# Streaming hybrid attention layer: in the last head unit the sample's tile is projected behind the sixteen token tiles instead of in front of them

## The chip, the core and the metric

The kernel runs on one core of a Trainium2 chip. The time is the device time of one execution in microseconds (us); before the change it is 2286.06 us, the median of three runs (2282.44 to 2286.41). The core has five engines with a queue of instructions each: PE (TensorE, matrix products), DVE (VectorE), ACT (ScalarE), POOL (GpSimd) and SP (SyncE, which here issues nearly all transfers). Each queue is worked off in the order in which the program holds it, and an instruction waits at the head of its queue until what it reads and writes is ready.

## The reference: what is computed

One layer of a streaming encoder. 2048 new token rows of one stream ("the prompt") and 8 x 16 rows of eight running streams ("the sample", 128 rows, which have cached keys and values) are normalised and modulated, and then projected by one wide weight matrix. Two mixers work side by side: differential attention with 4 heads (two softmaxes, the second subtracted with a factor) and stick-breaking attention with 8 heads:

    z     = q . k / 8                     # for keys before the query only
    log_a = log_sigmoid(z) + (reverse running sum of log_sigmoid(-z), without the own key)
    o     = exp(log_a) @ v

Behind them `y = x + gate * (sigmoid(ga) * ((norm(oa) * silu(za)) @ w_branch_a) + sigmoid(gb) * ((ob * silu(zb)) @ w_branch_b)) @ w_out`, normalised once more. The projected keys and values are outputs too, for the sample's rows as for the prompt's.

## The kernel before, in words

**Tiles and units.** The rows are cut into 17 tiles of 128: token tiles 0 to 15 and the sample's tile, which has number `NT` = 16. The heads are dealt to 8 units: even units hold one differential head, odd units two stick-breaking heads. Products are in float16 with a high and a low part, so a full product is three matmuls for each 128 rows of depth.

**Stage 0** (line 944) computes modulation and the normalised rows, and puts them, turned and split, into DRAM (`hT_d`).

**Stage 1** (lines 866 to 1357) goes through a list of steps `(unit, tile)`, `steps` in line 866. For a step two things have to be done.

- *The projection* (`project`, line 402): 24 matmuls of 128x512 (line 423) for q, k, v and the z gate, and in odd units another 24 (line 495) for a part of the merge gates. ACT, DVE and POOL bring the result to memory, split k, v and q, and transfers store z (`z_d`), gates (`g_d`) and outputs. For the sample's tile q, k, v also go to DRAM (`s_d`, lines 479, 480), and that is all that becomes of it in stage 1; a token tile is also turned by PE (`transpose_qk`, line 503, with two copies, lines 518 and 519) for its attention. The rows are fetched one step ahead into three buffers `hs`.
- *The attention* (token tiles only): `scores` (line 632) makes for query tile t one or two pieces of up to 512 keys at a time: two PE products (lines 647, 648), two sigmoids on ACT (line 549, 550, by the helper in line 120), a running product on DVE (line 607), and per 1024 keys a product on POOL (line 629), a cast on ACT (line 561), a difference on DVE (line 562) and a transposing transfer (line 568). `pv` (line 725) multiplies these weights with v on PE (lines 706, 707) at least `PV_LAG` = 2 steps later.

**The order.** All projections stand in one list, `line`: each step gives 24 pieces of two matmuls in odd units, and behind the sixth piece of a step stands the turning of the step before it, if that was a token tile. Before the change a last entry (line 901) turns the last token tile. The loop from line 1330 walks over n, one step of attention after the other. `attention(n)` gives the scores of step n and the v products of a step further back; `take` cuts the next pieces off `line`, so that the projection stands `LEAD` = 5 steps ahead of a pace which is counted in attention time: a token tile counts 0.6 + (t+1)/4, the sample's 0.3. `interleave` (line 92) merges pieces, scores and v products evenly, and the merged order is the program's. When `line` is used up, the entries of `cuts` (`early_work`, line 1306) are dealt out over the iterations that are left: one branch weight, one renaming of buffers (`rest`), `inputs` of the first two output tiles (`first`), four half branch products of tile 0 (`early` 0 to 3) and the transposing transfer of its result (`early` 4). Line 1354 takes the number of entries left over the number of iterations left, rounded up.

**Stage 2** (from line 1360) has output tiles 0 to 14, the sample's and 15. For each: `inputs` (line 1215) loads o, z and g (`hs` buffers 0 and 1 for o and z), takes sigmoids, products, a scale and a split into `hs` buffer 2; a transposing transfer (line 1251); four half branch products of 12 matmuls (line 1262); a second scale, split and transposing transfer (line 1287); two halves of 24 matmuls with `w_out` (line 1399), which is loaded at the start of this stage (line 1211) and kept; the last norm, and the store. The sample's attention over the caches is laid in between, unit by unit (`sample`, line 743).

**What fixes an order.** The helper `act` (line 118) makes every ACT instruction with a table function (sigmoid, exp) follow the one before it in the program. For everything else a planner lays the instructions of each engine out by a timeline of its own, with the program's order as the preference (line 1476: `schedule_with_timeline_sim=True`); waits on buffers and results are added by it. So an instruction can stand in its queue earlier or later than the loop wrote it.

**Buffers that are few.** v: 23 tiles (`V_BUFS`), k: 6 groups of four tiles (`K_BUFS`), turned q: 6 (`Q_BUFS`), PE result banks: 2 for `mm`, 3 for `s`, 1 for `t`, 2 for `o`. The sigmoids of z in `inputs` write the `mm` banks too. The buffers of stage 2 lie where those of stage 1 lay.

Of the kernel before, what the change touches and what calls it, by code (L numbers as in the profile page):

```python
# [32 lines left out]
NT = SEQ // P  # L33
# [77 lines left out]
def layer_kernel(ctx: ExitStack, tc: tile.TileContext, a: dict):  # L111
# [75 lines left out]
    def bank(tag, dt=F32):  # L187
        return ps.tile([P, 512 if dt == F32 else 1024], dt, tag=tag, name=f"ps_{tag}", bufs=BANKS[tag])
# [113 lines left out]
    units = [None] * 8  # L302
# [60 lines left out]
    def finish_unit(u):  # L363

        U = units[u]
        sw, sh = U["sw"], sh_box[0]
        sc = con.tile([P, 7], F32, name=f"usc{u}")

        V.tensor_tensor(out=sc[:, 0:1], in0=U["fsq"], in1=nh2, op=ALU.mult)
        sq = scales(sc[:, 0:1], con, f"sq{u}")  # L370

        V.tensor_tensor(out=sc[:, 1:2], in0=sw[:, 1:2], in1=sh[:, 1:2], op=ALU.mult)
        V.tensor_tensor(out=sc[:, 2:3], in0=sc[:, 1:2], in1=sq[:, 0:1], op=ALU.mult)

        V.tensor_scalar(out=sc[:, 3:4], in0=sq[:, 1:2], scalar1=sq[:, 1:2], scalar2=0.125, op0=ALU.mult, op1=ALU.mult)
        V.tensor_scalar(out=sc[:, 4:5], in0=sc[:, 3:4], scalar1=-1.0, scalar2=None, op0=ALU.mult)

        if U["kind"] == 0:
            V.tensor_tensor(out=sc[:, 5:6], in0=sq[:, 1:2], in1=ls[:, 1:2], op=ALU.mult)
        else:  # L380
            V.tensor_scalar(out=sc[:, 5:6], in0=sq[:, 1:2], scalar1=2.0 ** -STICK, scalar2=None, op0=ALU.mult)
        if "sg" in U:

            V.tensor_tensor(out=sc[:, 6:7], in0=U["sg"][:, 1:2], in1=sh[:, 1:2], op=ALU.mult)
        U["sc"], U["sq"], U["k"], U["v"] = sc, sq, {}, {}
# [11 lines left out]
    def fetch_h(u, t):  # L397
        ahead[u, t] = hs[len(fetched) % 3].bitcast(F16).rearrange("p (f k n) -> p f k n", f=2, n=P)
        fetched.append(t)
        load(out=ahead[u, t], in_=hT_d[t // 4][:, t % 4, :, :, :])  # L400
# [102 lines left out]
    def transpose_qk(U, t):  # L503
        g, i = t // 4, t % 4
        q16, k16 = U.pop(("q16", t)), U.pop(("k16", t))
        pt = bank("t", F16)
        for c in range(2):
            T.transpose(pt[:, c * P : (c + 1) * P], k16[:, c, :, :].rearrange("p f d -> p (f d)"), id16)
        for f in range(2):
            for c in range(2):  # L510
                j = 2 + f * 2 + c
                T.transpose(pt[:, j * P : (j + 1) * P], q16[:, f, c, :, :].rearrange("p r d -> p (r d)"), id16)
        if i == 0:
            U["k"][g] = kvp.tile([P, 2, 512], F16, tag="k", name="k", bufs=K_BUFS)
        U["q", t] = qst = stg.tile([P, 4, P], F16, tag="qst", name="qst", bufs=Q_BUFS)
        kst = U["k"][g][:, :, i * P : (i + 1) * P]
        copy = V.tensor_copy if U["kind"] == 1 else S.copy
        (V.tensor_copy if U["u"] == 0 else copy)(out=kst, in_=pt[:, 0:256].rearrange("p (c n) -> p c n", c=2))
        copy(out=qst, in_=pt[:, 256:768].rearrange("p (j n) -> p j n", j=4))
# [343 lines left out]

        return [lambda x=x: one(*x) for x in srcs]

    steps = [(u, t) for u in range(8) for t in [NT] + list(range(NT))]
    back = []
    spare = norms()
    jobs, done = [], []
# [1 line left out]

    line = []

    def begin(u, t):
        if t == NT:
            if u > 0:
                free.extend(units[u - 1]["bufs"])
            finish_unit(u)

    def projection(m):  # L880
        u, t = steps[m]
        made = []

        def piece(i):
            if i == 0:
                begin(u, t)
                made.extend(project(units[u], t))
            if i == H_AT and not at_hand and m + 1 < len(steps) and steps[m + 1] not in ahead:
                fetch_h(*steps[m + 1])
            made[i]()  # L890

        return [lambda i=i: piece(i) for i in range(12 + 3 * GATES[u][1] // 128)]

    starts = []
    for m in range(len(steps)):
        starts.append(len(line))
        for i, fn in enumerate(projection(m)):
            line.append((m, fn))
            if i == TR_AFTER and m > 0 and steps[m - 1][1] < NT:
                line.append((m - 1, lambda m=m: transpose_qk(units[steps[m - 1][0]], steps[m - 1][1])))  # L900
    line.append((len(steps) - 1, lambda: transpose_qk(units[7], NT - 1)))
    starts.append(len(line))
    at = [0]

# [425 lines left out]
    for n in range(first_step, len(steps) + PV_LAG):  # L1330
        if n < len(steps):
            u, t = steps[n]
# [147 lines left out]
```

## Time and profile before

| what | value |
|---|---|
| time, median of 3 runs | 2286.06 us |
| time of the profiled execution | 2285.48 us |
| its span, first to last instruction | 2283.7 us |
| PE busy | 2085.1 us (91%) |
| DVE busy | 1611.5 us (71%) |
| ACT busy | 1482.6 us (65%) |
| POOL busy | 688.1 us (30%) |
| mean granted PE clock | 0.966 |

A row of the profile's timeline gives start, duration, engine, line of the kernel, operation, the tile that is written and those that are read, shape and count; in square brackets stand the idle time of the engine before it and what ended it. Rows of windows give for a stretch of time the busy time of each engine (with counts), then the granted PE clock as a share of full speed, the busy share of the DMA engines and GB/s. Matmuls are pipelined, so the duration of one is longer than the distance between two.

### The profile page before, as it was taken

Reading aid. Unit: us, or ns where it says so; the run is one execution under the profiler, and the core shown is the slowest. Engines: PE = TensorE matmul, PEld = TensorE weight load, DVE = VectorE, ACT = ScalarE, POOL = GpSimd, SP = SyncE. Lnnn points to the kernel's source line nnn. Section 1 sums busy time; section 2 is a strip of 40 time slices with the busy share of each in tenths; the row PEclk is TensorE's granted clock in tenths of the full one; section 3 lists DMA queues with packets and bytes.
Section 4 is the critical chain, followed back from the end, with each engine's and each line's share of the span. In section 5 each row is a group of like instructions: output and inputs, shape, how many; then the busy total and the mean of one; then the engine's idle time right before and its main releaser. Section 6 shows DMA issues by size and latency. Waiting matters only on the chain. (4 is left out here: it accounts for less than half of the span.)

```text
span 2283.7 us, 40470 instructions
## 1 busy us (share of the span) xinstructions
PE 2085.1 (91%) x14478; PEld 1110.4 (49%) x14478; DVE 1611.5 (71%) x3507; ACT 1482.6 (65%) x2952; POOL 688.1 (30%) x559
## 2 busy tenths in 40 slices
PE   4997999999999999899999989999986799888997
PEld 2554554555555455455545555555543444444443
DVE  4668767789875778987577898776777656565554
ACT  3877677787876777786677777666776544444431
POOL 1522012355301335530032553012344232232321
PEclk7999999999999999999999999999997899999998
DMA  8667658697875778876566886757687989788652
GB/s 295 211 212 187 163 131 220 148 221 155 206 169 124 170 154 199 177 179 131 128 172 142 204 183 154 153 140 163 151 179 173 295 228 262 202 220 211 188 150 65
DMA packets 763754, 411.92 MB, mean 180 GB/s; under 512 B 524986, under 2 KB 708586, under 8 KB 763040
## 3 DMA queue, kind: packets, MB, share of 16 engines
q1 hardware_dynamic: 762474, 408.86, 72.6%
q8 instruction: 113, 1.85, 0.3%
q14 instruction: 89, 0.73, 0.1%
q10 hardware_dynamic: 1078, 0.48, 0.1%
HBM read 211.53 MB, written 72.91 MB: 125 GB/s over the span
## 5 line engine op out<-in xcount | busy, mean ns | idle before, releaser
L423 PE MATMUL ps_mm<-wb,hs 128*128 128x512 f16 x1836 | 460.7, 382 | 0.6 <-DVE v L292 0.5
L629 POOL TENSOR_TENSOR sc_p<-sc_p,sc_n 128x1024 f32<-128x1024 f32 (+8 forms) x160 | 278.1, 1742 | 459.2 <-DVE sc_n L607 451.6
L423 PEld LDWEIGHTS <-hs 128*128 128x128 f16 x2928 | 256.1, 98 | 226.9 <-issue 6.8
L607 DVE TENSOR_TENSOR_SCAN sc_n<-ps_s,sc_n,zero_t 128x512 f32<-128x512 f32 x192 | 245.3, 1278 | 64.4 <-ACT ps_s L120 62.2
L423 PE MATMUL ps_mm<-wa,hs 128*128 128x512 f16 x1092 | 279.4, 380 | 0.0
L647 PE MATMUL ps_s<-k,qst 128*128 128x512 f16 (+3 forms) x640 | 225.9, 354 | 38.3 <-DVE sc_n L607 30.1
L120 ACT ACTIVATE sc_p<-ps_s,usc 128x512 f32<-128x512 f32 (+3 forms) x320 | 202.0, 631 | 85.8 <-PE ps_s L648 55.1
L495 PE MATMUL ps_mm<-wa,hs 128*128 128x512 f16 x1020 | 257.0, 379 | 0.0
L562 DVE TENSOR_TENSOR sc_n<-sc_p,sc_n 128x1024 f16<-128x1024 f32 (+7 forms) x160 | 197.9, 1242 | 41.3 <-ACT sc_n L561 41.2
L648 PE MATMUL ps_s<-k,qst 128*128 128x512 f16 (+3 forms) x640 | 226.2, 354 | 0.0
L1399 PE MATMUL ps_o<-wo,wb 128*128 128x512 f16 x816 | 199.5, 401 | 24.7 <-DMA wb<-wa 22.0
L706 PE MATMUL ps_o<-v,wt 128*128 128x128 f16 x1008 | 175.6, 226 | 27.6 <-DMA wt<-sc_n 27.5
L495 PEld LDWEIGHTS <-hs 128*128 128x128 f16 x1632 | 140.2, 98 | 119.0
L120 ACT ACTIVATE ps_s<-ps_s,usc 128x512 f32<-128x512 f32 (+3 forms) x320 | 193.7, 605 | 0.0
L561 ACT CAST sc_n<-sc_p 128x1024 f16<-128x1024 f32 (+7 forms) x160 | 138.5, 870 | 49.2 <-POOL sc_p L629 49.1
L707 PE MATMUL ps_o<-v,wt 128*128 128x64 f16 x1008 | 158.5, 198 | 0.0
L495 PE MATMUL ps_mm<-wb,hs 128*128 128x512 f16 x612 | 155.9, 379 | 0.0
L706 PEld LDWEIGHTS <-wt 128*128 128x128 f16 x1008 | 99.2, 102 | 102.7 <-DMA wt<-sc_n 38.0
L1399 PEld LDWEIGHTS <-wb 128*128 128x128 f16 x816 | 82.1, 102 | 130.4 <-DMA wb<-wa 26.1
L457 POOL TENSOR_TENSOR rot<-pr,rope 128x256 f32<-128x256 f32 x68 | 63.1, 928 | 247.1 <-ACT pr L437 193.3
L437 ACT ACTIVATE pr<-ps_mm,usc 128x512 f32<-128x512 f32 (+1 forms) x136 | 86.5, 636 | 67.4 <-PE ps_mm L423 67.1
L545 DVE TENSOR_SCALAR_CACHE_REDUCE sc_n<-ps_s,usc 128x512 f32<-128x512 f32 (+3 forms) x148 | 99.0, 669 | 42.4 <-PE ps_s L648 28.2
(336 smaller groups left out, 4346.7 us busy)
## 6 DMA issues: line engine op xcount, KB each, us to landing
hs<-hT_d SPq DMA_DIRECT2D x122, 512.0 KB, 4.2
g_d<-gt SPq DMA_DIRECT2D x68, 256.0 KB, 3.4
out_dram<-pr SPq DMA_DIRECT2D x204, 64.0 KB, 1.8
wa<-g_d SPq DMA_DIRECT2D x25, 512.0 KB, 6.7
wide<-in_w_ada_dram SPq DMA_DIRECT2D x12, 1024.0 KB, 8.4
wa<-in_w_in_dram SPq DMA_DIRECT2D x44, 256.0 KB, 4.7
z_d<-pr SPq DMA_DIRECT2D x136, 64.0 KB, 2.7
o_d<-o SPq DMA_DIRECT2D x136, 64.0 KB, 2.7
```

Source lines behind the costliest of these rows:

```text
L120: i = S.activation(**kw)
L423: T.matmul(box["p"], box["h"][:, hi, k, :], U["w"][k][:, wi, :], start=(n == 0), stop=(n == 3 * KT - 1))
L495: T.matmul(box["g"][:, 0:gw], box["h"][:, hi, k, :], U["wg"][k // per][:, k % per, wi, :], start=(j == 0), stop=(j == 3 * KT - 1))
L561: S.copy(out=hi, in_=src)
L562: V.tensor_tensor(out=lo, in0=src, in1=hi, op=ALU.subtract)
L607: V.tensor_tensor_scan(out=dst[:, lo : lo + n][:, ::-1], data0=src[:, 0:n][:, ::-1], data1=zero_t[:, 0:1].to_broadcast([P, n]), initial=fi ...
L629: G.tensor_tensor(out=p[:, 0:m], in0=p[:, 0:m], in1=n[:, 1 : m + 1], op=ALU.mult)
L647: T.matmul(p[:, 0:n], qst[:, c, :], kk[:, c, 0:n], start=True, stop=False)
L648: T.matmul(p[:, 0:n], qst[:, 2 + c, :], kk[:, c, 0:n], start=False, stop=not diag)
L706: T.matmul(po[:, c * P : (c + 1) * P], wt[:, wj, :], vt[:, c, :, :], start=first, stop=False)
L707: T.matmul(po[:, c * P : c * P + 64], wt[:, nb + wj, :], vt[:, c, 0, :], start=False, stop=last)
L1399: T.matmul(po, st["y"][:, yi * 8 + k, :], wo[j * 4 + k // 2][:, wi, k % 2, :], start=(n == 0), stop=(n == 3 * KT - 1))
```

## The change

The list of steps has the sample's tile first in units 0 to 6, as before, and last in unit 7. `begin`, which frees the buffers of the unit before and makes the scales of the new one, ran when a step was the sample's; it now runs when the unit has no scales yet. As the last step is now the sample's, and behind the sixth piece of that step the turning of token tile 15 is written as for any other step, the extra last entry of `line` goes.

```diff
-    steps = [(u, t) for u in range(8) for t in [NT] + list(range(NT))]
+    steps = [(u, t) for u in range(7) for t in [NT] + list(range(NT))] + [(7, t) for t in range(NT + 1)]
...
-    def begin(u, t):
-        if t == NT:
+    def begin(u):
+        if "sc" not in units[u]:
             if u > 0:
                 free.extend(units[u - 1]["bufs"])
             finish_unit(u)
...
-                begin(u, t)
+                begin(u)
...
-    line.append((len(steps) - 1, lambda: transpose_qk(units[7], NT - 1)))
```

## The prediction

> **What bounds the kernel now.** I read the page's strips first, to find where PE, busy for 91% of the span, is not busy.
>
> ```profile
> span 2283.7 us, 40470 instructions
> ...
> PE   4997999999999999899999989999986799888997
> ...
> PEclk7999999999999999999999999999997899999998
> ```
>
> One slice is 57.1 us. Before slice 30 PE is full; slices 30 and 31 (1713 to 1827 us) are the one hole past the start. Windows of 50 and 20 us place it:
>
> ```profile
> 1600.00:1650.00 50.00, 50.00 (x338) 26.10 (x336) 35.22 (x57) 36.06 (x71) 16.20 (x13) 1.00 0.62 146
> ...
> 1700.00:1720.00 20.00, 12.54 (x94) 6.74 (x93) 17.58 (x19) 18.53 (x30) 13.61 (x7) 0.76 0.82 176
> 1720.00:1740.00 20.00, 10.10 (x76) 5.46 (x77) 19.73 (x25) 18.80 (x29) 7.41 (x4) 0.76 0.66 138
> 1740.00:1760.00 20.00, 13.51 (x96) 7.51 (x95) 14.87 (x24) 6.53 (x10) 8.68 (x5) 0.69 0.99 207
> ...
> 1780.00:1800.00 20.00, 11.83 (x42) 5.02 (x41) 10.57 (x17) 7.06 (x10) 2.81 (x3) 0.66 1.08 291
> ```
>
> Up to 1650 PE is saturated. From 1700 to 1740 DVE (19.73 of 20) and ACT (18.80) are, and PE idles half the time. From 1740 to 1760 nothing is: a chain of waits runs. At 1780 the DMA share is 1.08: stage 2 loads its weights. PE's timeline shows the seams:
>
> ```profile
> 1646.97 2.75 PE L423 MATMUL ps_mm<-wb,hs 128*128 128x512 f16 x12
> ...
> 1687.33 0.60 PE L495 MATMUL ps_mm<-wb,hs 128*128 128x512 f16 x2
> ...
> 1690.22 0.39 PE L512 MATMUL ps_t<-id,qbuf 128*128 128x128 f16 x4
> ...
> 1695.92 0.29 PE L706 MATMUL ps_o<-v,wt 128*128 128x128 f16 x1 [3.78 <-DMA wt<-sc_n]
> ...
> 1747.03 0.29 PE L706 MATMUL ps_o<-v,wt 128*128 128x128 f16 x1 [5.63 <-DMA wt<-sc_n]
> ...
> 1749.35 1.01 PE L1262 MATMUL ps_mm<-wa,wb 128*128 128x512 f16 x2 [0.86 <-DVE hs L1236]
> ...
> 1763.00 0.22 PE L706 MATMUL ps_o<-v,wt 128*128 128x128 f16 x1
> ...
> 1763.08 0.22 PE L706 MATMUL ps_o<-v,wt 128*128 128x128 f16 x1
> 1763.14 0.19 PE L707 MATMUL ps_o<-v,wt 128*128 128x64 f16 x1
> 1765.42 0.59 PE L1262 MATMUL ps_mm<-wa,wa 128*128 128x512 f16 x2 [2.08 <-DVE wa L1264]
> ```
>
> The last projection (1687.33) and the last turning (1690.22) end the cover; behind them attention of tiles 13 to 15 is alone, with waits for its weights. The half products of output tile 0 begin at 1749.35, the last v product ends at 1763.3.
>
> **What the change does to the order.** Attention time of a unit is 0.3 + 16 x 0.6 + 34 = 43.9, so 2.58 for each of 17 steps. Before, behind tile 12 there remain 4.1 + 4.35 + 4.6 = 13.05, or 5.05 steps: `line` stands at 136 - 5.05 + 5 = 135.95. Of the last step's 26 entries 25 are taken; tile 13 gets one, the turning of tile 15. After, 0.3 more remains (5.17 steps): 135.83, so 21 of 25 entries, and tile 13 gets the last four pieces of the sample, 8 matmuls. As the pace is counted in attention time, moving the sample costs or wins 0.116 of a step here, not a whole one. `cuts` begin at the same tile (14) but have five iterations instead of four, as one with no attention is left at the end: 9 entries go as 2, 2, 2, 2, 1 instead of 3, 2, 2, 2. The inputs of output tile 0 move from 0.83 of tile 14 to 0.25 of tile 15, those of tile 1 from 0.25 to 0.75 of tile 15; the half products move by one place, and the last transposing transfer of tile 0 stands behind everything.
>
> **T1, 8 matmuls into the hole.** Twelve take 2.75 us; less the 0.38 us tail of one, 11 distances are 2.37, so 0.2155 us each. Eight are 1.7 us which leave the saturated stretch for one in which PE idles 20 - 12.54 of 20 us. The turning goes the other way: four small ones take 0.39, one alone 0.22 (line 647 at 1523.59 below), so 0.057 apart, and six 0.3 us. -1.4 us; 0 if PE's idle time there is not used. What hides them is the wait of 3.78 us. The Trainium skill ("TensorE: Matmul & The Clock Gate", section "Part 1: The HAM clock gate") says that PE runs at half rate after about 3.4 us of idleness; the clock of 0.76 in the window agrees. By that rule the eight take 3.4 us in the hole, and were the hole not there, T1 would be +2.0 instead of -1.4.
>
> **T2, tile 15's two copies out of DVE's stretch.** The same pair in an earlier tile:
>
> ```profile
> 1525.22 0.27 DVE L518 COPY k<-ps_t 128x256 f16<-128x256 f16 x1
> ...
> 1525.60 0.42 DVE L519 COPY qst<-ps_t 128x512 f16<-128x512 f16 x1
> ```
>
> They move to tile 12, where PE is the bound. -0.7 to 0; I take -0.3, as DVE is near its bound only from 1700. The sample's projection leaves no k, v or q to be split, and its five stores are off any path; the count of matmuls and transfers is unchanged.
>
> **T3, the seam to unit 7.**
>
> ```profile
> 1517.09 0.38 PE L647 MATMUL ps_s<-k,qst 128*128 128x512 f16 x1
> ...
> 1523.59 0.22 PE L647 MATMUL ps_s<-k,qst 128*128 128x128 f16 x1
> ...
> 1533.16 0.27 PE L647 MATMUL ps_s<-k,qst 128*128 128x256 f16 x1 [0.27 <-DVE sc_n L655]
> ...
> 1542.68 0.23 PE L702 MATMUL ps_o<-v,wt 128*128 128x128 f16 x1 [1.84 <-DMA wt<-sc_n]
> ```
>
> Between the last scores of unit 6 (1517.09) and the first of unit 7 (1523.59) lies the step without scores. After, tile 0's scores stand in that iteration, and the v products of unit 6's last tile come one token tile later. PE's two waits, 0.27 and 1.84 us, can go or double: -2.1 to +2.1. I take -1.0, since the transfer waited for gets a tile more time. v tiles are no new wait: 16 of unit 6 and 6 of unit 7 are held at once, 22 of 23.
>
> **T4, the inputs of output tile 0, later.** The rows of ACT, DVE and SP:
>
> ```profile
> 1716.67 1.12 ACT L120 ACTIVATE ps_mm<-hs 128x512 f32<-128x512 f32 x2
> ...
> 1720.54 0.69 ACT L120 ACTIVATE sc_p<-ps_s,usc 128x512 f32<-128x512 f32 x1
> ...
> 1726.09 1.16 ACT L120 ACTIVATE ps_mm<-hs 128x512 f32<-128x512 f32 x2
> 1727.13 2.04 ACT L120 ACTIVATE wa<-wa 128x1024 f32<-128x1024 f32 x2
> ...
> 1736.51 0.78 ACT L120 ACTIVATE sc_p<-ps_s,usc 128x512 f32<-128x512 f32 x1
> ```
> ```profile
> 1734.90 3.02 DVE L292 SCALAR_TENSOR_TENSOR hs<-hs,su,hs 128x1024 f16<-128x1024 f32 x1
> ...
> 1753.09 1.28 DVE L292 SCALAR_TENSOR_TENSOR hs<-hs,su,hs 128x1024 f16<-128x1024 f32 x1
> ...
> 1777.37 0.74 DVE L292 SCALAR_TENSOR_TENSOR wa<-wa,sy,wa 128x512 f16<-128x512 f32 x1
> ```
> ```profile
> 1713.28 7.18 SPq L568 DMA_TRANSPOSE wt<-sc_n  x3
> 1720.57 1.10 SPq L1219 DMA_DIRECT2D hs<-z_d  x1
> ...
> 1739.99 0.93 SPq L1218 DMA_DIRECT2D hs<-o_d  x1
> ...
> 1753.23 1.97 SPq L568 DMA_TRANSPOSE wt<-sc_n  x1
> ...
> 1759.42 4.31 SPq L1211 DMA_DIRECT2D x<-in_w_out_dram  x2
> ...
> 1782.74 5.91 SPq L1287 DMA_TRANSPOSE wb<-wa  x1
> ```
>
> `act` ties all sigmoids to the program's order. Three pairs of tiles 14 and 15 (from 1720.54 to the next inputs at 1726.09, 5.5 us) now stand ahead of tile 0's sigmoids: 1716.67 becomes 1722.2. Tile 1's 3 us (1726.09 to 1729.17) now stand before the pair at 1736.51, so at 1733.5; the sum ahead of the last two pairs is the same, and they stay. Behind tile 0's sigmoids run scale, split (to 1737.92), load of tile 1's o into the buffer that it frees (1739.99), its products, and so the banks for the first half product (1749.35). Moved by 5.5 us this starts at 1754.9. The four halves are 48 x 0.2155 = 10.3 us, to 1765.2 against 1763.3, where they have v products among them that can now run in the gap ahead. So 1.9 us at the seam. Behind it tile 0's second split ends at 1778.11, while SP issues its transfer (L1287) only at 1782.74: 4.6 us of slack. 0 to +5.5; I take +1.5, near the 1.9, little of it absorbed.
>
> A second split of the same size took 1.28 us and this one 3.02, with a POOL product beside it from 1734.01. The Trainium skill ("SBUF — State Buffer", section "SBUF: two separate sides") holds that DVE and POOL share a port pair that one locks for a whole instruction; by it a moved split that no longer meets POOL saves 1.7 us and T4 is -0.2.
>
> **Sum.** -1.4 - 0.3 - 1.0 + 1.5 = -1.2 us on the execution profiled, 2285.48 us (span 2283.7 and 1.8 around it): 2284.3. That execution is 0.6 under the median, so this is no change: 0.2% is 4.6 us, about what a measurement can tell (the three runs span 4.0).
>
> **Rivals.**
>
> *A, faster.* The last v products no longer queue behind the halves. Of the transposing transfers of weights the trace says:
>
> ```profile
> DMA to landing us min/median/max: 2.4/4.3/8.3
> ```
>
> The last weights are issued from 1753.23 to 1755.20 and their products ended after the halves, 1763.3; with the median of 4.3 us they could be used at 1759.5 and done by 1760.7, as blocks stand 0.08 us apart (1763.00 to 1763.08) and 12 to 16 of them take 1.0 to 1.3. The second `w_out` load (L1211, 4.31 us for two issues, so the second near 1763.3) waits for that end: -2.6. With T1, T2 and T3 at their low ends (-4.2) and T4 at 0: -6.8, 2278.7. For it: the 2.08 us wait at 1765.42 and the load-bound stretch at 1780. Against: `w_out` loads also follow each other through two buffers.
>
> *B, slower.* Tile 1's sigmoids become a gate. They need z of tile 1 (L1219), which may load only when tile 0's z is read, and on SP it can stand behind transposing transfers; three of them held SP 7.18 us at 1713.28. The load comes 3.9 us after tile 0's sigmoids now; moved it is issued at 1726.1 and, with the 4.3 us above, lands at 1730.4, 3.1 before its use at 1733.5. From that point on every us holds ACT, and by `act` also the last two pairs of tile 15, their weights and the v products behind. With the full 7.18 it is 4.1 us, on top of T4 at 5.5: 9.6 - 1.4 - 0.3 = +7.9, 2293.4. Against: the planner may issue z first.
>
> *C, it does not do what it says.* The planner lays engines out by its own timeline; the halves already stand far behind their place (written beside tile 15's scores, run at 1749.35). If it did the same with everything moved, nothing changes: 2285.5.
>
> **Chances and range.** The forecast 0.33, C 0.12, A 0.31, B 0.24. Faster by over 0.2% is A, slower is B, within is forecast and C: 0.31, 0.24, 0.45. The likeliest one's own range is 2281.3 (T1 to T3 low, T4 at 0) to 2290.6 (0.2% up). A and B reach 2278.7 and 2293.4; some room for unknown planner moves in stage 2 gives 2274 to 2295.
>
> **What would show it.** T1: eight L495 matmuls behind the first scores of tile 13. T3: first unit 7 scores among unit 6's v products, no wait over 1 us near 1540. T4: tile 0's z sigmoids near 1722, its first half product near 1755, L1287 at most 2 us later. A: the last L707 before the last half product of tile 0. B: an ACT idle of over 1 us ahead of tile 1's sigmoids. I am wrong if stage 2, from the first L1399 to the end, changes its own length by more than 4 us, since I hold it fixed.

## The result, and the profile after

The change makes the kernel slower by a little: 2291.46 us after (median of 20 runs, 2286.83 to 2297.55) against 2286.11 us before (20 runs, 2281.45 to 2290.92). The ratio is 1.0025 with a 95% interval of 1.0016 to 1.0033, that is +3.7 to +7.5 us. The profiled execution took 2289.78 us (span 2288.0). One of the twelve executions of e3 below took 3616.18 us at a granted clock of 0.559 and is left out of that run's figures. Lines behind 901 stand one lower than before: L1399 is now L1398, L1287 is L1286, L1251 is L1250, L1413 is L1412.

The page of the kernel after, its strips:

```profile
span 2288.0 us, 40462 instructions
...
PE   4997999998999999899999989999986788888997
...
PEclk7998999999999999999999999999987899999998
```

Busy time by windows, kernel after (PE, PEld, DVE, ACT, POOL, then granted clock, DMA share, GB/s):

```profile
1700.00:1720.00 20.00, 12.63 (x97) 7.20 (x96) 17.48 (x17) 17.35 (x29) 13.98 (x7) 0.76 1.03 204
1720.00:1740.00 20.00, 10.66 (x86) 6.11 (x84) 19.12 (x28) 20.00 (x32) 8.81 (x4) 0.67 0.63 133
1740.00:1760.00 20.00, 11.70 (x81) 6.71 (x80) 11.32 (x19) 4.57 (x7) 7.81 (x8) 0.61 0.85 186
...
1826.00:1900.00 74.00, 63.03 (x534) 34.16 (x532) 42.74 (x111) 35.38 (x69) 19.89 (x15) 0.97 0.84 223
1900.00:2270.00 370.00, 334.38 (x2226) 166.33 (x2225) 201.44 (x545) 144.97 (x273) 103.88 (x78) 0.96 0.72 188
```

The same two last windows of the kernel before:

```profile
1826.00:1900.00 74.00, 68.25 (x556) 36.27 (x555) 42.51 (x114) 34.04 (x65) 22.00 (x16) 0.95 0.87 230
1900.00:2270.00 370.00, 333.74 (x2215) 165.74 (x2213) 200.07 (x543) 144.59 (x273) 102.09 (x78) 0.96 0.72 187
```

From 1700 to 1760 PE's busy time in the two kernels is 1.2 us apart (36.2 before, 35.0 after). Between 1826 and 1900, PE of the kernel after is busy 5.2 us less (63.03 against 68.25), and behind 1900 the two are equal again. So the time goes in a stretch of stage 2 that lies 60 us behind the end of the edited code. The stores of the output tiles are milestones. First and fourth store, before and then after:

```profile
1826.53 0.36 SPq L1413 DMA_DIRECT2D out_dram<-x  x1
...
1921.21 0.36 SPq L1413 DMA_DIRECT2D out_dram<-x  x1
```
```profile
1826.11 0.36 SPq L1412 DMA_DIRECT2D out_dram<-x  x1
...
1927.37 0.38 SPq L1412 DMA_DIRECT2D out_dram<-x  x1
```

At the first store the kernel after is 0.4 us ahead; at the fourth it is 6.2 us behind, and at the end of the span 4.3. From first to fourth store: 94.7 us before, 101.3 after.

PE's waits in this stretch, before and then after (all over 0.9 us up to 1900, and the start of the output products near 1897):

```profile
1853.41 0.63 PE L777 MATMUL ps_s<-ident,dk 128*128 128x128 f32 x4 [2.91 <-DVE dsc L607]
...
1874.49 0.66 PE L777 MATMUL ps_t<-ident,dk 128*128 128x128 f32 x4 [1.80 <-DVE dks L778]
...
1897.03 2.33 PE L1399 MATMUL ps_o<-wo,wb 128*128 128x512 f16 x10 [0.57 <-DMA wb<-wa]
```
```profile
1835.09 0.66 PE L777 MATMUL ps_t<-ident,dk 128*128 128x128 f32 x4 [2.85 <-DVE dks L778]
...
1857.04 2.33 PE L1398 MATMUL ps_o<-wo,wb 128*128 128x512 f16 x7 [3.08 <-DMA wb<-wa]
...
1899.06 1.46 PE L1398 MATMUL ps_o<-wo,wb 128*128 128x512 f16 x3 [4.44 <-DMA wb<-wa]
```

Together 5.3 us before and 10.4 after: 5.1 us more, about the PE time that is missing. They are other waits, at other places. The second one after is for y of the third output tile, whose transfer is issued at 1852.63 instead of 1849.89. The last one is for y of the fourth output tile, and SP's queue shows why it is late. Before, and then after:

```profile
1873.87 6.22 SPq L1251 DMA_TRANSPOSE wa<-hs  x1
1880.55 1.02 SPq L758 DMA_DIRECT2D dv<-in_cache_a_v_dram  x2
1881.68 1.00 SPq L696 DMA_DIRECT2D o_d<-o  x1
...
1888.62 6.43 SPq L1287 DMA_TRANSPOSE wb<-wa  x1
```
```profile
1882.19 3.08 SPq L758 DMA_DIRECT2D dv<-in_cache_a_v_dram  x2
1885.38 1.74 SPq L696 DMA_DIRECT2D o_d<-o  x1
1887.22 1.89 SPq L758 DMA_DIRECT2D dv<-in_cache_a_v_dram  x2
1889.20 5.35 SPq L1250 DMA_TRANSPOSE wa<-hs  x1
1894.65 1.83 SPq L1286 DMA_TRANSPOSE wb<-wa  x1
```

The transposing transfer of u of the sixth output tile (L1251, now L1250) stood ahead of four loads of the sample's cached values (dv) and a store; now it stands behind them, 15.3 us later, and the transfer of y (L1286) 6.0 us later. The first wait has another cause. DVE and ACT of the kernel after:

```profile
1831.82 1.12 DVE L1235 SCALAR_TENSOR_TENSOR hs<-ps_mm,orms,hs 128x128 f32<-128x128 f32 x4 [4.10 <-ACT ps_mm L120]
...
1834.35 0.68 DVE L778 COPY dks<-ps_t 128x512 f32<-128x512 f32 x1
```
```profile
1828.18 0.63 ACT L274 ACTIVATE junk<-wb 128x512 f16<-128x512 f32 x1 [5.37 <-POOL wb L1265]
...
1831.13 0.60 ACT L120 ACTIVATE ps_mm<-hs 128x512 f32<-128x512 f32 x1
```

DVE stands 4.1 us in front of products of the fifth output tile (L1235) that need a sigmoid, which stands on ACT behind a sum that itself waited 5.4 us; behind L1235 on DVE stands the copy of the sample's keys (L778) that PE wants. In the kernel before the same copy stands ahead of those products:

```profile
1827.33 0.69 DVE L778 COPY dks<-ps_t 128x512 f32<-128x512 f32 x1 [0.16 <-PE ps_t L777]
...
1829.38 1.13 DVE L1236 SCALAR_TENSOR_TENSOR hs<-ps_mm,orms,hs 128x128 f32<-128x128 f32 x4 [1.35 <-POOL hs L1230]
```

The Trainium skill ("PSUM — Partial Sum Buffer", section "Engine vs sequencer instructions") states that the queues of ScalarE and VectorE are strictly first in, first out. These rows agree: the copy starts at 1834.35, behind the products that waited.

Stage 2's program text is the same in both kernels, instruction for instruction. What differs is the order in which the planner laid it into the queues: 36 of SP's 220 places in stage 2, 158 of DVE's 744, 44 of ACT's 303, 13 of POOL's 112, 617 of PE's 15121. On SP they all lie ahead of the transfer of y of the fifth output tile (1919.83 after).

### The profile page after: what moved, and what is told of

The parts are those of the page before. It is cut to its first block, busy times and chain, and to the rows that moved or that the text cites. A ratio compares the mean times of both kernels' runs of the same rounds, so it can differ in the third digit from the quotient of the medians.

```text
span 2288.0 us, 40462 instructions
## 1 busy us (share of the span) xinstructions
PE 2081.9 (91%) x14478; PEld 1110.6 (49%) x14478; DVE 1609.4 (70%) x3507; ACT 1483.1 (65%) x2952; POOL 692.1 (30%) x559
## 5 line engine op out<-in xcount | busy, mean ns | idle before, releaser
L1398 PE MATMUL ps_o<-wo,wb 128*128 128x512 f16 x816 | 199.3, 399 | 29.3 <-DMA wb<-wa 24.2
L706 PEld LDWEIGHTS <-wt 128*128 128x128 f16 x1008 | 100.4, 103 | 110.7 <-DMA wt<-sc_n 45.1
L1398 PEld LDWEIGHTS <-wb 128*128 128x128 f16 x816 | 81.8, 102 | 134.2 <-DMA wb<-wa 28.8
L707 PEld LDWEIGHTS <-wt 128*128 128x128 f16 x1008 | 98.3, 101 | 64.1 <-issue 1.1
```

Source lines behind the costliest of these rows:

```text
L706: T.matmul(po[:, c * P : (c + 1) * P], wt[:, wj, :], vt[:, c, :, :], start=first, stop=False)
L707: T.matmul(po[:, c * P : c * P + 64], wt[:, nb + wj, :], vt[:, c, 0, :], start=False, stop=last)
L1398: T.matmul(po, st["y"][:, yi * 8 + k, :], wo[j * 4 + k // 2][:, wi, k % 2, :], start=(n == 0), stop=(n == 3 * KT - 1))
```

## The experiments

Theory P says that this other order costs the 5 us. Its rivals: T, the later inputs of output tiles 0 and 1 cost it; M, the sample's projection at its new place costs it in stage 1. The order can be forced without a wait: a list of stage 2's instructions for each queue, each told to stand behind the one before it. The pinned kernels have two lines more ahead of the code, so L1398 of the kernel after is L1400 there. The lists come from one of the two kernels, as each diff says: BEFORE and AFTER stand there for the packed lists. Each run has 5 to 12 executions, and the kernel before was timed 23 to 35 times beside them. A profile is one execution and can lie some us from the median of its run (e2's and e14's 5.4 and 6.4 us above, e5's 7.0 below).

| run | what | ratio to before, 95% interval |
|---|---|---|
| e1 | after, order of before | 0.9995 (0.9983 to 1.0007) |
| e2 | before, order of after | 1.0035 (1.0023 to 1.0048) |
| e3 | before, dealt 2, 2, 2, 3 | 1.0023 (1.0011 to 1.0035) |
| e4 | after, dealt 3, 2, 2, 2 | 1.0025 (1.0014 to 1.0035) |
| e5 | after, u ahead on SP | 1.0016 (1.0004 to 1.0029) |
| e6 | before, u behind on SP | 0.9996 (0.9986 to 1.0006) |
| e7 | after, u and y ahead on SP | 1.0012 (1.0002 to 1.0021) |
| e8 | before, y ahead on SP | 1.0029 (1.0018 to 1.0039) |
| e9 | after, SP's order of before | 1.0025 (1.0014 to 1.0035) |
| e10 | after, the engines' order of before | 1.0054 (1.0039 to 1.0069) |
| e11 | after, DVE, ACT, POOL of before | 1.0087 (1.0069 to 1.0106) |
| e12 | after, two places on SP | 1.0013 (1.0003 to 1.0022) |
| e13 | after, order of before behind first store | 0.9998 (0.9989 to 1.0007) |
| e14 | after, order of before ahead of it | 1.0024 (1.0013 to 1.0035) |
| e15 | projection moved alone, order of before | 0.9991 (0.9980 to 1.0002) |
| e16 | later hand-over alone, order of before | 1.0001 (0.9993 to 1.0010) |
| e17 | after, order of before, first to second store | 1.0021 (1.0012 to 1.0031) |
| e18 | after, order of before behind second store | 1.0015 (1.0005 to 1.0025) |

### Is it the order? (e1 to e4)

```diff
+STAGE2_ORDER = {...}
...
+    live = {i.name: i for i in nc.cur_bb.bb.instructions}
+    for packed in STAGE2_ORDER.values():
+        last = None
+        for n in json.loads(zlib.decompress(base64.b85decode(packed))):
+            i = live.get(f"I-{n}")
...
+            if last is not None:
+                tc.add_manual_dep(i, last.name, NOSYNC, reason="stage 2 order")
+            last = i
```

e1 is the kernel after with the five lists of before; e2 the kernel before with the five lists of after.

> The kernel after, with nothing changed but the order in which each engine's and SP's queue takes the instructions of stage 2 (the weights of w_out and all behind them), which is forced to the order that the kernel before has. Theory P (the time is lost because stage 2's queues, SP's above all, come out in another order): no slower than before, 2282 to 2288 us, and the first transposing transfer (u) of the sixth output tile is back near 1874 us instead of 1889. Theory T (tile 0's and tile 1's inputs are handed over later at the end of unit 7): still 2289 to 2293. Theory M (the projection of the sample at its new place costs it in stage 1): still 2289 to 2293.

> The kernel before, with stage 2's queues forced to the order that the kernel after has; stage 1 and the dealing of its last work are those of before. Theory P: 2289 to 2293 us, slower by the 5.4 us of the change. Theory T: 2284 to 2288, as the inputs of output tiles 0 and 1 come as early as before. Theory M: 2284 to 2288.

e3 is the kernel before, dealt as after:

```diff
-            pieces = [(1.0, fn) for fn in cuts[: -(-len(cuts) // (len(steps) + PV_LAG - n))]]
+            pieces = [(1.0, fn) for fn in cuts[: 2 if n < len(steps) + PV_LAG - 1 else len(cuts)]]
```

> The kernel before, the sample's projection in front of the token tiles as before, but the nine entries at the end of unit 7 are dealt 2, 2, 2, 3 instead of 3, 2, 2, 2: the inputs of output tiles 0 and 1 come as late as in the kernel after. Its stage 2 comes out with exactly the order of the kernel after on all queues. Theory P: 2289 to 2293 us. Theory T: 2289 to 2293 too, and the first y store at 1829 or later, against 1826.5 before. Theory M: 2284 to 2288.

e4 is the kernel after, dealt as before:

```diff
-            pieces = [(1.0, fn) for fn in cuts[: -(-len(cuts) // (len(steps) + PV_LAG - n))]]
+            pieces = [(1.0, fn) for fn in cuts[: -(-len(cuts) // (max(1, len(steps) + PV_LAG - 1 - n)))]]
```

> The kernel after, but its nine entries are dealt 3, 2, 2, 2, 0 over the iterations, as before the change. Its stage 2 comes out in a third order (63 of SP's 220 places differ from either kernel's). Theory P gives no time, only that what it gains or loses against before arises behind the first y store (about 1826 us): 2280 to 2295. Theory T: 2284 to 2288, as the inputs come early again. Theory M: 2289 to 2293.

Measured: e1 2282.91 us with everything that the change does to stage 1 (before in the same series 2283.82); the sixth u is issued at 1876.0. e2 2291.62 us. So the order alone carries the loss, in both directions; T and M, which expect e1 to stay slow, fall with e1, and M with e3 too. The traces show the same from first to fourth store: 94.6 us in e1, 100.9 in e2, 99.8 in e3. No run pins a kernel to its own order, but e3 has the loss without any list, so the forcing isn't its cause. e2's profile, an execution above its median, has one more wait, where early inputs meet an order made for late ones:

```profile
1777.47 1.01 PE L1264 MATMUL ps_mm<-wa,wa 128*128 128x512 f16 x2 [8.09 <-DVE hs L1238]
```

e3, 2291.02 us, has the sample's projection in front, as before, and yet stage 2 in exactly the order of the kernel after on all five queues. So the dealing of nine entries at the end of unit 7 is enough to make the planner choose that order. The moved projection is not neutral either: e4, with the old dealing, has a third order and takes 2290.57 us. Its loss arises elsewhere, which is not what theory P had expected of it: the first store comes at 1841.85, 15.3 us later than before, and from there to the fourth it takes 89.4 us, 5.3 less than before. So e4 decides nothing about T. Neither dealing that was run with the projection moved gave the order of before by itself.

### Is it one place on SP? (e5 to e8)

The numbers name instructions of stage 2: 22690 is the transfer of u of the sixth output tile, 22617 that of y of the fourth, 22359, 22444, 22567 and 22619 the dv loads, 22565 the o_d store, 22614 the load dsam, 22616 and 22689 dk loads, 22759 an o load. In each pair the first stands behind the second. e5, e6, e7 and e8:

```diff
+    for later, first in [(22359, 22690), (22444, 22359), (22565, 22444), (22567, 22565), (22619, 22567), (22617, 22619)]:
+        tc.add_manual_dep(live[f"I-{later}"], f"I-{first}", NOSYNC, reason="SP order")
```

> The kernel after with one transfer moved on SP alone: the transposing transfer of u of the sixth output tile is issued ahead of four dv loads and one o_d store of the sample instead of behind them, as it stands in the kernel before; all other queues keep the order of the kernel after. Theory S (this one place on SP costs the 5 us): 2283 to 2288 us, u issued at 1880 to 1885 instead of 1889.2, and the wait of 4.44 us for y (at 1899) gone or under 1 us. Theory D (the loss is spread over the orders of DVE, ACT, POOL and PE): 2289 to 2293.

```diff
+    for later, first in [(22359, 22616), (22444, 22359), (22565, 22444), (22567, 22565), (22614, 22567), (22619, 22614), (22689, 22619), (22690, 22689), (22759, 22690), (22617, 22759)]:
```

> The kernel before with the same one transfer moved the other way on SP: u of the sixth output tile behind the four dv loads and the o_d store, as it stands in the kernel after; all other queues as before. Theory S: 2287 to 2292 us, a wait of 3 us or more for y ahead of the output products near 1897. Theory D: 2281 to 2286, no change.

```diff
+    for later, first in [(22617, 22690), (22359, 22617), (22444, 22359), (22565, 22444), (22567, 22565), (22619, 22567)]:
```

> The kernel after with two transfers moved on SP: u of the sixth and y of the fourth output tile, both ahead of the four dv loads and the o_d store. Theory S: as far as the products wait for y alone, 2280 to 2285 us, y issued near 1887 instead of 1894.7; but the sample's values come 5 us later, and if PE's next work is theirs, that takes the gain back: 2285 to 2289. Theory D: 2289 to 2293.

```diff
+    for later, first in [(22617, 22690), (22359, 22617), (22444, 22359), (22565, 22444), (22567, 22565), (22614, 22567), (22619, 22614)]:
```

> The kernel before with y of the fourth output tile moved ahead of the four dv loads and the o_d store on SP (u of the sixth stands there already). Theory S: 2278 to 2284 us if PE still loses time to that y transfer (its products start at 1897.0, y issued at 1888.6 while its buffer is free from 1882.6), 2284 to 2288 if the sample's values are then late. Theory D: 2281 to 2286.

Theory S, one place on SP, falls with e6. There u is issued 10.1 us later than before (at 1883.96) and the kernel takes 2283.87 us, no slower: the output products waited 1.27 us in place of 0.57. e5 wins about 2 of the 5.7 us by the middle of its interval, but that interval (a loss of 0.9 to 6.6 us) allows that it wins nearly all or nothing; its wait for y is still 3.98 us. (That profile took 2281.43 us, the fastest of e5's twelve: a wait seen in one trace isn't yet a loss.) e7 wins about 3, again by the middle. e8, which puts y ahead of the sample's values in the kernel before, costs 6.6 us, more than either theory allowed: y is issued 6.1 us earlier, and later the sample's work is late instead. In e8:

```profile
1923.52 0.69 PE L763 MATMUL ps_t<-ident,dsam 128*128 128x128 f32 x2 [3.96 <-DVE dks L778]
```

So the row that catches the eye, 15.3 us late, is worth nothing in one kernel and, by the middle of a wide interval, less than half of the loss in the other.

### Which queue? (e9 to e12)

All four pin all five queues; the lists differ.

```diff
+STAGE2_ORDER = {"SP": BEFORE, "PE": AFTER, "DVE": AFTER, "Activation": AFTER, "Pool": AFTER}
```

> The kernel after with SP alone in the stage 2 order of the kernel before (36 of 220 places); PE, DVE, ACT and POOL keep the stage 2 order of the kernel after. Theory S2 (the loss lies in SP's order as a whole, at several places): 2282 to 2287 us. Theory E (it lies in the engines' own order): 2287.5 to 2292, little won.

```diff
+STAGE2_ORDER = {"SP": AFTER, "PE": BEFORE, "DVE": BEFORE, "Activation": BEFORE, "Pool": BEFORE}
```

> The kernel after with PE, DVE, ACT and POOL in the stage 2 order of the kernel before, and SP alone in that of the kernel after: the other half of the same cut. Theory S2: 2288 to 2293 us, little won. Theory E: 2282 to 2287. If neither half wins it, the orders only fit together as pairs.

```diff
+STAGE2_ORDER = {"SP": AFTER, "PE": AFTER, "DVE": BEFORE, "Activation": BEFORE, "Pool": BEFORE}
```

> The kernel after with DVE, ACT and POOL in the stage 2 order of the kernel before; SP and PE in that of the kernel after. Theory E, if DVE, ACT or POOL carry it: 2282 to 2287 us; if PE's order carries it, or by theory S2: 2288.5 to 2293.

```diff
+STAGE2_ORDER = {"SP": AFTER, "PE": AFTER, "DVE": AFTER, "Activation": AFTER, "Pool": AFTER}
+sp.remove(22411); sp.insert(sp.index(22140) + 1, 22411)
+sp.remove(22690); sp.insert(sp.index(22359), 22690)
```

> The kernel after with two moves on SP, all else in its own order: u of the sixth output tile ahead of the four dv loads and the o_d store, and the z load of the fifth output tile, which waits at 1833.7 us for its buffer, behind one dk load and the dsam load instead of in front of them (both as in the kernel before). Theory S2, if these two places are the loss: 2283 to 2287 us, and PE's wait of 2.85 us at 1835 for the dk split shorter by 2 us or more. Otherwise 2287 to 2291, as with the first of the two alone.

Neither half wins it: SP alone 2290.36 us, the engines alone 2297.89, DVE, ACT and POOL alone 2304.71. S2 falls and E falls, and e10 and e11 are slower than any theory had them; the case that e10's expectation names last holds, the orders only fit together. My reading, not tested by a run of its own, is that SP brings things in one order and the engines ask for them in another. The longest waits of these profiles between 1826 and 1930 us speak for it, that for y in e9 and that for a load of keys in e11:

```profile
1900.02 1.46 PE L1400 MATMUL ps_o<-wo,wb 128*128 128x512 f16 x3 [7.75 <-DMA wb<-wa]
```
```profile
1885.88 1.08 PE L779 MATMUL ps_s<-ident,dk 128*128 128x128 f32 x4 [8.01 <-DMA dk<-in_cache_a_k_dram]
```

e12, two moves on SP (the z load, 22411, is the sixth output tile's, not the fifth's as its expectation says), takes 2286.82 us, within theory S2's range: by the middle half of the loss is back, as with e5 and e7, and the three intervals overlap. But the sign that S2 named is missing: PE's wait at 1835, 2.85 us in the kernel after, is 2.87 (at 1838.21), and that for y 4.29.

### Which stretch? (e13, e14, e17, e18)

The lists are cut at the first y store (near 1826 us) and at the second (near 1862), at places where each queue has issued the same instructions in both orders. The three parts of each list, in this order: up to the first store, up to the second, the rest.

```diff
+STAGE2_ORDER = AFTER, BEFORE, BEFORE
```

> The kernel after; all five queues keep its own order of stage 2 up to the first y store (near 1826 us) and have that of the kernel before from there on. Theory L (the loss arises behind the first y store, between 1826 and 1900, as the traces of before and after show it): 2282 to 2287 us. Theory F (the order of the first stretch starts it, and the rest only follows): 2288.5 to 2293.

```diff
+STAGE2_ORDER = BEFORE, AFTER, AFTER
```

> The kernel after; all five queues have the order of the kernel before up to the first y store and keep their own from there on: the other half. Theory L: 2288.5 to 2293 us. Theory F: 2282 to 2287.

```diff
+STAGE2_ORDER = AFTER, BEFORE, AFTER
```

> The kernel after; between the first and the second y store (about 1826 to 1862 us) the five queues have the order of the kernel before, ahead of it and behind it their own. Theory V (the loss arises behind the second y store, at the y and u transfers near 1890): 2288 to 2293 us. Theory Z (it arises between the two stores, where z's load holds up the sample's keys, and only shows later): 2282 to 2287. If both share it: 2286 to 2289.

```diff
+STAGE2_ORDER = AFTER, AFTER, BEFORE
```

> The kernel after; up to the second y store (about 1862 us) the five queues have its own order, behind it that of the kernel before. Theory V: 2282 to 2287 us, and PE's wait of 4.44 us for y at 1899 gone or under 1.5 us. Theory Z: 2288 to 2293. If both share it: 2286 to 2289.

Theory L holds: with the order of before from the first store on, 2285.42 us, with it only ahead of that, 2292.43. In the windows of e13 PE's busy time is back:

```profile
1826.00:1900.00 74.00, 67.32 (x547) 34.87 (x546) 41.37 (x113) 35.30 (x69) 23.24 (x17) 0.95 0.88 229
```

and its largest wait from 1826 to 1900 is the one that the kernel before has too (1874.49):

```profile
1876.34 0.66 PE L779 MATMUL ps_t<-ident,dk 128*128 128x128 f32 x4 [1.82 <-DVE dks L780]
```

e14 keeps both waits for y that the kernel after has:

```profile
1864.71 3.17 PE L1400 MATMUL ps_o<-wo,wb 128*128 128x512 f16 x7 [3.76 <-DMA wb<-wa]
...
1907.12 1.46 PE L1400 MATMUL ps_o<-wo,wb 128*128 128x512 f16 x3 [4.85 <-DMA wb<-wa]
```

The second cut settles less. The stretch between the first and the second store alone wins little (2292.33 us against 2286.78 before in that series), the stretch behind it alone some 2 of the 5 us (2289.81), both together all of it. So e17 came out as theory V said and e18 did not: there the wait for y is 2.63 us, over the 1.5 that V named, and a wait of 3.41 us stands near 1836 as in the kernel after. By the middles of the intervals the parts don't add up, though the intervals leave room. Which positions carry the rest stays open.

### The two edits alone (e15, e16)

e15 is e4's kernel, e16 is e3's, both with the five lists of before.

```diff
+            pieces = [(1.0, fn) for fn in cuts[: -(-len(cuts) // (max(1, len(steps) + PV_LAG - 1 - n)))]]
...
+STAGE2_ORDER = BEFORE
```

> The moved projection alone: the kernel after, with the nine entries dealt 3, 2, 2, 2 as before, and stage 2 in the order of the kernel before. By the terms of the prediction T1, T2 and T3 remain: -2.7 us, 2281 to 2283 (bounds -4.2 to +2.1: 2280 to 2286). If the projection's place is worth nothing: 2284 to 2286.

```diff
+            pieces = [(1.0, fn) for fn in cuts[: 2 if n < len(steps) + PV_LAG - 1 else len(cuts)]]
...
+STAGE2_ORDER = BEFORE
```

> The later hand-over alone: the kernel before, with the nine entries dealt 2, 2, 2, 3, and stage 2 in the order of the kernel before. By the prediction's term T4 +1.5 us (bounds 0 to +5.5): 2285 to 2287, and up to 2291 if it is not absorbed. If the late inputs are hidden: 2283 to 2285.

The moved projection: 2283.37 us, -2.1 us (-4.6 to +0.5). The later hand-over: +0.2 us (-1.6 to +2.3) by the ratio. e1, both together: -1.1 us (-3.9 to +1.6). From first to fourth store e15 takes 94.6 us and e16 95.6, as the kernel before does (94.7). With e1 this leaves nothing for T or M: both edits stand there, and the loss is gone.

## Why the prediction was wrong

The direction was wrong; that the sizes of the edits were wrong too isn't shown. The sum of T1 to T4 was -1.2 us; e1, which runs all of them with stage 2 held, measured -1.1, and e15 and e16 measured -2.1 and +0.2 for -2.7 and +1.5. The intervals are too wide to confirm a term of one or two us; they do exclude that the edits cost 5. The step that failed is the one that stands last in the prediction: "I hold it fixed", of stage 2's own length. From the first output product (1790.65 before, 1790.03 after) to the end of the span stage 2 took 493.1 us before and 498.0 after, 4.9 more, over the 4 us named there. The two starts, before and then after:

```profile
1790.65 2.74 PE L1399 MATMUL ps_o<-wo,wb 128*128 128x512 f16 x6 [6.10 <-DMA wb<-wa]
```
```profile
1790.03 3.39 PE L1398 MATMUL ps_o<-wo,wb 128*128 128x512 f16 x8 [2.36 <-DMA wb<-wa]
```

What the runs showed in its place: the planner laid stage 2 out in another order, and that order alone costs 0.35% (e2) and its return wins everything back (e1). No rival covers it: C let the planner undo the change, none let it lay out anew a stage that the change doesn't touch; "some room for unknown planner moves" widened the range, without a chance for slower. That 2291.46 lies inside 2274 to 2295 is owed to this room and to B, whose wait didn't come; it is no credit to the mechanism. A first price stood in the trace: the waits of 2.91 and 1.80 us show a stretch without slack. That is hindsight, and no bound: e11 lost 20 us to a mixed order.

Point by point:

**T1** went as described. The eight matmuls in the kernel after, the first and the last pair:

```profile
1686.15 0.59 PE L495 MATMUL ps_mm<-wb,hs 128*128 128x512 f16 x2
...
1690.44 0.59 PE L495 MATMUL ps_mm<-wb,hs 128*128 128x512 f16 x2
1695.32 0.29 PE L706 MATMUL ps_o<-v,wt 128*128 128x128 f16 x1 [3.75 <-DMA wt<-sc_n]
```

They stand among the scores of tile 13, 0.22 us apart as before, so the 3.4 us that the prediction set against them at half rate didn't come, and the wait behind them is 3.75 us as before (3.78). That they shift time from the full stretch into the hole isn't seen apart from T3.

**T2**: the copies of tile 15 moved as said: the last pair on DVE stands at 1680.30 and 1680.50 instead of 1690.65 and 1690.86. No run shows its -0.3 by itself.

**T3**: unit 7's first scores come at 1520.69 instead of 1523.59, the wait of 0.27 us became 0.59, and that of 1.84 for a transfer is gone; in its place PE waits 0.98 us for ACT:

```profile
1520.69 0.22 PE L647 MATMUL ps_s<-k,qst 128*128 128x128 f16 x1
...
1533.77 0.27 PE L647 MATMUL ps_s<-k,qst 128*128 128x256 f16 x1 [0.59 <-DVE sc_n L655]
...
1536.19 2.75 PE L423 MATMUL ps_mm<-wb,hs 128*128 128x512 f16 x12 [0.98 <-ACT gt L498]
```

No wait over 1 us, as forecast; 0.5 us less waiting where -1.0 was taken.

**T4**: the order came out as worked out, the end of it did not. POOL of the kernel before, then ACT, DVE, POOL, PE and SP of the kernel after:

```profile
1734.01 2.83 POOL L629 TENSOR_TENSOR sc_p<-sc_p,sc_n 128x1024 f32<-128x1024 f32 x1 [2.94 <-DVE sc_n L607]
```

```profile
1722.20 1.14 ACT L120 ACTIVATE ps_mm<-hs 128x512 f32<-128x512 f32 x2
...
1732.63 1.20 ACT L120 ACTIVATE ps_mm<-hs 128x512 f32<-128x512 f32 x2
```
```profile
1740.45 1.25 DVE L292 SCALAR_TENSOR_TENSOR hs<-hs,su,hs 128x1024 f16<-128x1024 f32 x1
...
1741.89 4.01 DVE L562 TENSOR_TENSOR sc_n<-sc_p,sc_n 128x1024 f16<-128x1024 f32 x2
```
```profile
1740.67 2.89 POOL L629 TENSOR_TENSOR sc_p<-sc_p,sc_n 128x1024 f32<-128x1024 f32 x1 [2.42 <-DVE sc_n L607]
```
```profile
1751.81 1.04 PE L1261 MATMUL ps_mm<-wa,wb 128*128 128x512 f16 x2
```
```profile
1782.76 5.26 SPq L1286 DMA_TRANSPOSE wb<-wa  x1
```

Tile 0's sigmoids start at 1722.20 (forecast 1722.2), but the split ends at 1741.70, 3.8 us later than before instead of 5.5, because it took 1.25 us, not 3.02. Before, POOL's product had begun 0.9 us ahead of it; now DVE begins first. The sentence on the Trainium skill ("SBUF — State Buffer", section "SBUF: two separate sides") bears on just this: which of the two starts first holds the shared ports for a whole instruction. DVE's two durations agree with it; POOL's 2.89 us, against 2.83 before, shows no wait of POOL's in turn. The meeting with POOL isn't gone, though: DVE's next product, which starts while POOL's is running, takes 2.75 us (its row counts its successor in), against 1.23 for the same shape at 1738.10. The half products start at 1751.81, not near 1755. The forecast also took all 48 at 0.2155 us; the first six before and the first eight after stand about 0.43 us apart, at a granted clock of 0.69 and 0.61 in that window. The transfer that had 4.6 us of slack (L1286) is issued at 1782.76, 0.02 later than before. So this trace shows nothing of the 1.5 us, though e16's interval doesn't exclude it.

**A** showed its sign without its gain: the last v products end at 1762.3, before the last half product, yet the wait behind them grew from 2.08 to 2.90 us, and at the first store the execution is 0.4 us ahead. **B** didn't come: no idle time of ACT stands ahead of tile 1's sigmoids at 1732.63, which the forecast had at 1733.5.

## What to carry to other kernels

Where a planner lays out the queues, a change can move the order of any later code whose timeline it touches, the same program text included: give that a chance in a forecast, and not only room in the range. The waits of the tightest stretch downstream (here 5 us) are a first price: a better order can win about as much there (e4's stretch was 5.3 us shorter), a worse one can lose far more (20 us in e11). To find out what an edit itself is worth, hold the order of everything else and time it again; and where the order is the cause, don't expect one row to carry it: compare whole orders, cut by time rather than by queue. Here some queues in one order and the rest in the other were no faster than the slower whole order (e9) or slower than both (e10, e11).

## What was not expected

That orders mixed by queue can cost more than either whole one: with DVE, ACT and POOL in one order and SP and PE in the other the kernel takes 2304.71 us, 0.9% over before. And that a transposing transfer which is issued 10.1 us later (e6) can cost nothing, while one that is issued 6.1 us earlier (e8) can cost 6.6 us (0.0029 x 2285.25; 4.1 to 8.9 by the interval).
